# Weight forms of a pair kept in less space outside the FFN, and three more pairs in the 7-product form, in a streaming-encoder layer in split fp32

## The chip, the cores and the metric

The kernel runs on one core of one Trainium2 chip. The metric is the device time of one execution in microseconds (us). Before the change it is 1463.98 us, the median of three runs (1463.22 to 1464.94). One more execution was recorded by the profiler; it took 1464.63 us.

## What is computed

One layer of a hybrid encoder, with x of 256 rows (S) and 2048 columns (D), all in fp32. Cut to what matters:

```python
def reference(x, p, w_in, w_sb_out, w_ca_out, w_mix_out, rel_bias, g_mix, g_ffn, ...):
        h = rmsnorm(x, g_mix[i])
        proj = h @ w_in[i]
        q_sb, k_sb, v_sb, q_ca, k_ca, v_ca, gate_sb, gate_ca = jnp.split(proj, splits, axis=-1)
        y_sb = stick_breaking_attention(q_sb, k_sb, v_sb)
        y_ca = chunked_relpos_attention(q_ca, k_ca, v_ca, rel_bias[i])
        merged = (jax.nn.sigmoid(gate_sb) * (y_sb @ w_sb_out[i])
                  + jax.nn.sigmoid(gate_ca) * (y_ca @ w_ca_out[i]))
        x = x + merged @ w_mix_out[i]
        h = rmsnorm(x, g_ffn[i])
        g_ff, u_ff = jnp.split(h @ w_ffn_in[i], 2, axis=-1)
        x = x + (jax.nn.silu(g_ff) * u_ff) @ w_ffn_out[i]
        h = rmsnorm(x, g_ple[i])
        x = x + jax.nn.sigmoid(h @ w_ple_gate[i]) * (p[i] @ w_ple_in[i])
    return rmsnorm(x, g_final)
```

The two gates have 2048 columns each, w_mix_out is 2048 x 2048, and the FFN's hidden width is 5632.

## The kernel before

**Products in three parts.** Every operand of a big product is held as two fp32r tiles: hi, the value cast to fp32r, and lo, what the cast left over. A product is three matmuls (`three`, L267 to L270): hi·hi, hi·lo, lo·hi. The rows of x are the stationary operand, in tables T1, T2 or T3 of hi and lo by k-tile (128 rows of the contraction); the weights stream past in 512 columns. The weights arrive in fp32 in "raw" tiles of 128x1024, 512 KB each (L205, issued by SP in order, five buffers by turns, RAW = 5). ACT casts raw to hi (L239), DVE subtracts to get lo (`minus`, L221). There are three hi/lo buffers, and a fourth while the gates run (`extra`).

**Units.** A unit takes two blocks of 512 output columns over all k-tiles, two at a time: for 16 k-tiles, eight pairs. An ordinary pair is two pieces (one per block) of 12 matmuls each. A pair whose number is in `pairs` takes the 7-product form of a 2x2 block product (`pair_products`): seven products of three matmuls, 21 for 24. It needs extra forms of both sides. On the side of x these are sums of blocks of a table (`sums_of`), made once per table by `pair_sums` or by `into_table` and kept in FP (two slots before) or in a part of another tile (`F_gate`). On the side of the weights `split_pair` makes them for each pair: with raw1 and raw2 the raw tiles of the two k-tile rows, DVE makes t3 into xf, changes a block of raw2 in place, makes t2 and t4 into xf, and subtracts two lo of 1024 columns and one of 1536; ACT casts two hi and one of 1536 (L254, L257, L260). The 1536-wide hi and lo go to a "room" of 3072 columns. Four of the seven products are summed in PSUM tiles of their own (`su`). After the last such pair, `mid` adds those sums into the unit's output tile: one copy by ACT (L796) and four additions by DVE (L798), "su adds" here. At the unit's end `add_sums` (L802) adds the four PSUM tiles of the blocks, the "mm adds". Four mm tiles and two su tiles take turns, so the next unit's matmuls into one wait for the add that reads it.

**Stages.** The attention's projections and the two attentions come first. Then the gates: the first 512 columns of both as ordinary groups, then three units c=1, 2, 3, each with pairs 2, 4 and 6, all with one room, the tile that x had. Then the groups with w_sb_out and w_ca_out (the "out groups"), which multiply by the gates and put the sum into T1 (`into_table`, key "mg"). Then two mix units on w_mix_out, with pairs 4 and 6 only (MIX_PAIRS). Then the FFN in units with pairs 2, 4 and 6, the last norm's gate and the final norm.

**Order.** The program runs through `flush`: `prefetch` loads raw tiles as buffers come free and splits up to three pieces ahead; `tasks` are small jobs that are put between pieces. A scheduler then orders each engine's instructions ahead of time; on the chip each engine, SP's queue included, takes them strictly in that order. A raw tile's buffer is loaded again once the last instruction that reads it is done.

## Time and profile before

| what | value |
|---|---|
| median of three runs | 1463.98 us |
| profiled execution | 1464.63 us |
| its span, first to last instruction | 1462.9 us |
| TensorE's granted clock, mean | 0.998 |
| PE busy | 1450.5 us |
| DVE busy | 1211.8 us |
| ACT busy | 797.3 us |
| gate units c=1, c=2, c=3 | about 354 to 396, 396 to 438, 438 to 480 us |
| out groups, mix units, FFN | about 480 to 574, 574 to 655, from 655 us |

The profiled execution is 0.65 us above the median. PE is TensorE's matmuls, PEld its weight loads, DVE VectorE, ACT ScalarE, SP the queue that issues loads. In a timeline row the columns are start in us, duration in us, engine, line, operation, output<-inputs, shapes, the number of instructions that the row joins, and in brackets the idle time before it and what ended it. A row of a group gives count, busy us, mean ns of one, and idle time before by releaser. Matmuls overlap, so their durations are longer than the step from one start to the next.

### The profile page before, as it was taken

Reading aid. Unit: us, or ns where it says so; the run is one execution under the profiler, and the core shown is the slowest. Engines: PE = TensorE matmul, PEld = TensorE weight load, DVE = VectorE, ACT = ScalarE, POOL = GpSimd, SP = SyncE. Lnnn points to the kernel's source line nnn. Section 1 sums busy time; section 2 is a strip of 40 time slices with the busy share of each in tenths; the row PEclk is TensorE's granted clock in tenths of the full one; section 3 lists DMA queues with packets and bytes.
Section 4 is the critical chain, followed back from the end, with each engine's and each line's share of the span. In section 5 each row is a group of like instructions: output and inputs, shape, how many; then the busy total and the mean of one; then the engine's idle time right before and its main releaser. Section 6 shows DMA issues by size and latency. Waiting matters only on the chain.

```text
span 1462.9 us, 18648 instructions
## 1 busy us (share of the span) xinstructions
PE 1450.5 (99%) x6871; PEld 1214.2 (83%) x6871; DVE 1211.8 (83%) x1521; ACT 797.3 (55%) x949; POOL 23.5 (2%) x45
## 2 busy tenths in 40 slices
PE   9999999999999999999999999999999999999997
PEld 7888888888888888888888888888888888888886
DVE  5666667796888667988999999999999999999775
ACT  6455555457555444555555555555644555655652
POOL 0200000000000000000000000000000000000000
PEclk9999999999999999999999999999999999999999
DMA  9965555565666766666666566666666666666772
GB/s 297 294 186 173 173 173 176 179 194 160 214 196 206 236 189 190 207 191 183 188 189 203 184 205 203 200 211 210 192 191 213 188 203 194 207 203 200 235 230 97
DMA packets 164732, 291.19 MB, mean 199 GB/s; under 512 B 9024, under 2 KB 42096, under 8 KB 164384
## 3 DMA queue, kind: packets, MB, share of 16 engines
q1 hardware_dynamic: 162528, 281.32, 61.5%
q0 software_dynamic: 2112, 8.68, 1.9%
q8 instruction: 54, 0.88, 0.3%
q14 instruction: 38, 0.31, 0.1%
HBM read 284.19 MB, written 5.77 MB: 198 GB/s over the span
## 4 chain that ended last, share of the span: by engine, by line
PE 95%; DVE 2%; DMA 1%; issue 1%; ACT 0%; POOL 0%; POOLq 0%; DVEq 0%; ACTq 0%
PE mm L269 23%; PE mm L270 23%; PE mm L268 23%; PE mm L335 8%; PE mm L337 4%; PE su L268 3%; PE su L270 3%; PE su L269 3%; PE tp L413 1%; DMA raw<-in_w_ffn_out 1%; DVE lo L221 1%; DMA raw<-in_w_ple_gate 0%; PE warm L506 0%; PE yp L634 0%; PE xps L467 0%
## 5 line engine op out<-in xcount | busy, mean ns | idle before, releaser
L221 DVE TENSOR_TENSOR lo<-raw,hi 128x1024 fp32r<-128x1024 f32 (+1 forms) x517 | 626.8, 1220 | 147.0 <-ACT hi L239 144.0
L239 ACT CAST hi<-raw 128x1024 fp32r<-128x1024 f32 (+1 forms) x399 | 418.1, 1051 | 363.5 <-PE mm L270 233.7
L269 PE MATMUL mm<-lo,T 128*128 128x512 f32 x1391 | 542.7, 391 | 0.9 <-DVE lo L221 0.9
L270 PE MATMUL mm<-hi,T 128*128 128x512 f32 x1391 | 540.5, 390 | 0.0
L268 PE MATMUL mm<-hi,T 128*128 128x512 f32 x1391 | 516.8, 391 | 0.0
L269 PEld LDWEIGHTS mm<-lo,T 128*128 128x128 f32 x1391 | 261.2, 188 | 54.5 <-DVE lo L221 1.3
L270 PEld LDWEIGHTS mm<-hi,T 128*128 128x128 f32 x1391 | 261.2, 188 | 53.6
L268 PEld LDWEIGHTS mm<-hi,T 128*128 128x128 f32 x1391 | 261.0, 188 | 53.0
L335 PE MATMUL mm<-T,hi 128*128 128x512 f32 x512 | 180.3, 398 | 0.0
L337 PE MATMUL mm<-T,lo 128*128 128x256 f32 x512 | 141.0, 280 | 0.0
L257 ACT CAST hi<-raw 128x1024 fp32r<-128x1024 f32 x59 | 62.1, 1053 | 106.6 <-DVE raw L221 53.9
L335 PEld LDWEIGHTS mm<-T,hi 128*128 128x128 f32 x512 | 95.4, 188 | 21.5
L221 DVE TENSOR_TENSOR xf<-raw 128x512 f32<-128x512 f32 x118 | 81.1, 688 | 22.4 <-DMA raw<-in_w_in 5.6
L221 DVE TENSOR_TENSOR T<-xf,T 128x1536 fp32r<-128x1536 f32 x50 | 87.9, 1757 | 13.3 <-ACT T L260 12.8
L337 PEld LDWEIGHTS mm<-T,lo 128*128 128x128 f32 x512 | 96.3, 189 | 1.1
L260 ACT CAST T<-xf 128x1536 fp32r<-128x1536 f32 x50 | 74.1, 1481 | 30.0 <-DVE xf L221 29.8
L254 ACT CAST hi<-raw 128x1024 fp32r<-128x1024 f32 x59 | 62.1, 1053 | 22.5 <-PE mm L270 12.9
L798 DVE TENSOR_TENSOR C<-su,C 128x512 f32<-128x512 f32 x72 | 47.8, 685 | 4.6 <-PE su L270 3.2
L802 DVE TENSOR_TENSOR C<-mm,C 128x512 f32<-128x512 f32 x72 | 47.9, 684 | 2.8 <-PE mm L270 2.8
L221 DVE TENSOR_TENSOR xf<-raw,xf 128x512 f32<-128x512 f32 x59 | 40.5, 687 | 0.6
L221 DVE TENSOR_TENSOR raw<-raw 128x512 f32<-128x512 f32 x59 | 40.4, 685 | 0.2
L268 PE MATMUL mm<-T,T 128*128 128x512 f32 (+1 forms) x82 | 30.2, 368 | 0.0
(301 smaller groups left out, 1373.0 us busy)
## 6 DMA issues: line engine op xcount, KB each, us to landing
raw<-in_w_ffn_in SPq DMA_DIRECT2D x176, 512.0 KB, 4.2
raw<-in_w_in SPq DMA_DIRECT2D x160, 512.0 KB, 3.7
raw<-in_w_ffn_out SPq DMA_DIRECT2D x88, 512.0 KB, 4.8
raw<-in_w_mix_out SPq DMA_DIRECT2D x32, 512.0 KB, 4.4
raw<-in_w_ple_gate SPq DMA_DIRECT2D x32, 512.0 KB, 5.0
raw<-in_w_sb_out SPq DMA_DIRECT2D x16, 512.0 KB, 4.7
raw<-in_w_ca_out SPq DMA_DIRECT2D x16, 512.0 KB, 4.4
x<-in_x SPq DMA_DIRECT2D x4, 512.0 KB, 9.9
```

The lines of the kernel that those rows point to most:

```text
L221: nc.vector.tensor_tensor(out, a, b, ALU.subtract)
L239: nc.scalar.copy(hi[:, c : c + m], raw[:, c : c + m])
L254: nc.scalar.copy(h1, raw1)
L257: nc.scalar.copy(h2, raw2)
L260: nc.scalar.copy(xh, xf)
L268: nc.tensor.matmul(ps, xh, hi, start=a, stop=False)
L269: nc.tensor.matmul(ps, xh, lo, start=False, stop=False)
L270: state["mm"] = nc.tensor.matmul(ps, xl, hi, start=False, stop=z)
L335: nc.tensor.matmul(ps, hi[:, i, f], lhs[:, kt, :, :].rearrange("p c s -> p (c s)"), start=a, stop=False)
L337: nc.tensor.matmul(ps[:, :S], lo[:, i, f], lhs[:, kt, 0, :], start=False, stop=z)
L798: nc.vector.tensor_tensor(C[i], q, C[j], ALU.add)
L802: nc.vector.tensor_tensor(g["C"][i], g["ps"][i], g["C"][i], ALU.add)
```

## The change

While `late` has no pool, which is in the gates (the mix units and the FFN split their pairs with it, as before), `split_pair` works in less space. Only t3 goes to an xf of 512 columns; t2 and t4 overwrite the two blocks of raw1, once lo of raw1 is made, and raw1 as it then stands is cast and subtracted for the two extra forms; t3's forms have a tile x3 of 1024 columns. So one operation more is needed on DVE and on ACT per pair, and raw1 is read until the pair's last subtraction. The two raw tiles' blocks are named b11, b21, b12, b22. A room is then 3 x 1024 columns, and the gates get two by turns: thirds of `room`, and three tiles `more` in buffers that the attention has left. FP has three slots, the fourth set of forms is in the rest of `room`. With these, the mix units use pairs 2, 4 and 6, and gate unit c=3 uses pairs 1, 2, 4 and 6. The pending tasks are run before the sums for the gates, and those for pair 1 are a task.

```diff
-MIX_PAIRS = (4, 6)
+LAST_PAIRS = (1, 2, 4, 6)
...
-    FP = bp.tile([P, 2, 2, 4, P], F32R, tag="FP", name="FP")
+    FP = bp.tile([P, 3, 2, 4, P], F32R, tag="FP", name="FP")
...
+        if pool is not None:
+            xl, xh = room[:, :1536], room[:, 1536:]
+            xf = pool.tile([P, 1536], F32, tag="xf", name="xf")
...
+        else:
+            xh, xl, x3 = room
+            t3 = bp.tile([P, NB], F32, tag="xf", name="xf")
+            minus(t3, b22, b12)
+            minus(b12, b12, b11)
+            minus(l1, raw1, h1.bitcast(F32))
+            nc.scalar.copy(h2, raw2)
+            minus(b11, b22, b12)
+            minus(b21, b21, b11)
+            nc.scalar.copy(xh, raw1)
+            nc.scalar.copy(x3[:, :NB], t3)
+            minus(l2, raw2, h2.bitcast(F32))
+            minus(xl, raw1, xh.bitcast(F32))
+            minus(x3[:, NB:], t3, x3.bitcast(F32)[:, :NB])
...
+    while tasks:
+        run_task()
+    more = tuple(mp.tile([P, 1024], F32R, tag=tag, name="more") for tag in ("qT", "kT", "v"))
+    gate_rooms = [tuple(room[:, o : o + 1024] for o in (0, 1024, 2048)), more]
+    F_gate = dict(zip(PAIRS + (1,), F_gate))
+    for pair in PAIRS:
+        pair_sums(T1, 2 * pair, F_gate[pair])
+    tasks.append((None, lambda: pair_sums(T1, 2, F_gate[1])))
     for c in range(1, 4):
...
+             gate_rooms, lambda c=c: gate_slots(c), mid, add_sums, hneed, alone=True, pairs=PAIRS if c < 3 else LAST_PAIRS)
...
-                later(lambda: into_table(T1, c, mg, key="mg", forms=lambda kt: FP[:, kt // 4 - 2], pairs=MIX_PAIRS))
+                later(lambda: into_table(T1, c, mg, key="mg", forms=lambda kt: FP[:, kt // 4 - 1]))
...
-        unit(w_mix_out[0], (c * NB, (c + 1) * NB), range(KD), T1, lambda kt: FP[:, kt // 4 - 2], mix_rooms, C_slots,
-             mid, mix_post(c), lambda kt: ("mg", kt), pairs=MIX_PAIRS)
+        unit(w_mix_out[0], (c * NB, (c + 1) * NB), range(KD), T1, lambda kt: FP[:, kt // 4 - 1], mix_rooms, C_slots,
+             mid, mix_post(c), lambda kt: ("mg", kt))
```

Counted in the order lists, PE goes from 6828 to 6819 instructions, DVE has 36 more (10 in the mix units and 5 in their table, 6 in the new pair of c=3, 9 in the old gate pairs, 6 in pair 1's sums), ACT has 16 more. SP's loads keep their order and number. Up to the gates and in the last part of the kernel the lists are the same; from the gates to the end of the FFN they differ.

First place: pair 6 of gate unit c=2 on DVE, before. raw_3839 and raw_3841 are its two raw tiles; the other lo belong to pieces around it.

```order
L221 TENSOR_TENSOR xf_3888<-raw_3841 128x512
L221 TENSOR_TENSOR lo_2973<-raw_3785,hi_2972 128x1024
L221 TENSOR_TENSOR raw_3841<-raw_3841,raw_3839 128x512
L221 TENSOR_TENSOR lo_3890<-raw_3839,hi_3889 128x1024
L221 TENSOR_TENSOR xf_3888<-raw_3841 128x512
L221 TENSOR_TENSOR lo_3892<-raw_3841,hi_3891 128x1024
L221 TENSOR_TENSOR xf_3888<-raw_3839,xf_3888 128x512
L221 TENSOR_TENSOR room_2971<-xf_3888,room_2971 128x1536
L221 TENSOR_TENSOR lo_3920<-raw_3843,hi_3919 128x1024
```

The same pair after; its raw tiles are raw_3859 and raw_3861.

```order
L221 TENSOR_TENSOR xf_3913<-raw_3861 128x512
L221 TENSOR_TENSOR lo_2973<-raw_3803,hi_2972 128x1024
L221 TENSOR_TENSOR raw_3861<-raw_3861,raw_3859 128x512
L221 TENSOR_TENSOR lo_3909<-raw_3859,hi_3908 128x1024
L221 TENSOR_TENSOR room_2971<-xf_3913,room_2971 128x512
L221 TENSOR_TENSOR lo_3911<-raw_3861,hi_3910 128x1024
L221 TENSOR_TENSOR raw_3859<-raw_3861 128x512
L221 TENSOR_TENSOR raw_3859<-raw_3859 128x512
L221 TENSOR_TENSOR lo_3940<-raw_3863,hi_3939 128x1024
L221 TENSOR_TENSOR room_2971<-raw_3859,room_2971 128x1024
```

The 1536-wide subtraction became a 512-wide one early and a 1024-wide one at the end, which is the last to read raw_3859, and the lo of the next piece stands ahead of it. The buffer that it frees is raw_3957's, which the second place uses.

Second place: DVE at the end of unit c=2, before. gates<-su are the su adds, gates<-mm the mm adds of c=2; the raw tiles belong to c=3.

```order
L221 TENSOR_TENSOR lo_3966<-raw_3886,hi_3965 128x1024
L221 TENSOR_TENSOR lo_3970<-raw_3915,hi_3969 128x1024
L798 TENSOR_TENSOR gates_518<-su1_3790,gates_518 128x512 x2
L798 TENSOR_TENSOR gates_518<-su0_3789,gates_518 128x512 x2
L802 TENSOR_TENSOR gates_518<-mm0_3708,gates_518 128x512
L221 TENSOR_TENSOR xf_4043<-raw_3989 128x512
L802 TENSOR_TENSOR gates_518<-mm1_3709,gates_518 128x512
L221 TENSOR_TENSOR lo_3994<-raw_3917,hi_3993 128x1024
L802 TENSOR_TENSOR gates_518<-mm0_3722,gates_518 128x512
```

And after:

```order
L221 TENSOR_TENSOR xf_4032<-raw_3957 128x512
L221 TENSOR_TENSOR lo_3992<-raw_3937,hi_3991 128x1024
L221 TENSOR_TENSOR raw_3957<-raw_3957,raw_3955 128x512
L221 TENSOR_TENSOR more_3352<-xf_4032,more_3352 128x512
L816 TENSOR_TENSOR gates_518<-su1_3808,gates_518 128x512
L221 TENSOR_TENSOR xf_4079<-raw_4011 128x512
L816 TENSOR_TENSOR gates_518<-su1_3808,gates_518 128x512
L820 TENSOR_TENSOR gates_518<-mm0_3724,gates_518 128x512
L221 TENSOR_TENSOR raw_4011<-raw_4011,raw_4009 128x512
L221 TENSOR_TENSOR lo_4030<-raw_3955,hi_4029 128x1024
L816 TENSOR_TENSOR gates_518<-su0_3807,gates_518 128x512 x2
L221 TENSOR_TENSOR room_2971<-xf_4079,room_2971 128x512
```

Two xf, of c=3's pairs 1 and 2, and the work on their raw tiles stand ahead of and among the su adds. The four rows behind this piece are lo_2973<-raw_3957, raw_3955<-raw_3957, and the mm adds of mm1_3725 and mm1_3739.

Third place: PE at the start of unit c=3 after, nine matmuls from the second and then the eight behind them. Before, this stretch holds ordinary pieces only, into mm tiles; now pair 1's products stand in it.

```order
L286 MATMUL mm0_4044<-hi_3987,T1_71 128x512
L287 MATMUL mm0_4044<-lo_3988,T1_71 128x512
L288 MATMUL mm0_4044<-hi_3987,T1_71 128x512
L286 MATMUL mm0_4044<-hi_3987,T1_71 128x512
L287 MATMUL mm0_4044<-lo_3988,T1_71 128x512
L288 MATMUL mm0_4044<-hi_3987,T1_71 128x512
L286 MATMUL mm0_4044<-hi_4029,T1_71 128x512
L287 MATMUL su0_4091<-lo_4030,T1_71 128x512
L288 MATMUL su0_4091<-hi_4029,T1_71 128x512
```

```order
L287 MATMUL mm0_4044<-lo_4030,T1_71 128x512
L288 MATMUL mm0_4044<-hi_4029,T1_71 128x512
L286 MATMUL su0_4091<-hi_2972,room_2971 128x512
L286 MATMUL mm0_4044<-hi_4074,T1_71 128x512
L287 MATMUL su0_4091<-lo_2973,room_2971 128x512
L288 MATMUL su0_4091<-hi_2972,room_2971 128x512
L286 MATMUL su0_4091<-hi_4074,T1_71 128x512
L286 MATMUL mm1_4045<-hi_3987,T1_71 128x512
```

Matmuls on lo_4030 and lo_2973, the two lo that pair 1 needs, stand ninth and fifteenth in the unit; the first into mm0_4044 waits for the add that reads mm0_3724, and the one into mm1_4045 for the add that reads mm1_3725.

38 lines of the change are left out of this document (18 added, 20 removed).

## The prediction

> **What bounds the kernel now.** I read the page's busy line and chain first, then what PE waited for, then a table of stages, and last the rows of the places that the change touches.
>
> ```profile
> PE 1450.5 (99%) x6871; PEld 1214.2 (83%) x6871; DVE 1211.8 (83%) x1521; ACT 797.3 (55%) x949; POOL 23.5 (2%) x45
> PE 95%; DVE 2%; DMA 1%; issue 1%; ACT 0%; POOL 0%; POOLq 0%; DVEq 0%; ACTq 0%
> PE warm L506 <- POOL mhalf L97: 1.2, 1, 1.2
> PE mm L268 <- ACT hi L239: 1.2, 1, 1.2
> PE mm L269 <- DVE lo L221: 0.9, 1, 0.9
> ```
>
> PE is busy for 99% of the span and is 95% of the chain. It waits three times, 3.3 us in all. So there is no wait to win back here; only fewer matmuls can shorten the chain, and each new wait of PE lengthens it at full price. The stages (PE, PEld, DVE, ACT, POOL, then the granted clock, DMA share and GB/s) are gate units c=2 and c=3, the start of the mix, its second unit, and a stretch of the FFN:
>
> ```profile
> 396.00:438.00 42.00, 42.00 (x187) 34.77 (x186) 36.40 (x40) 24.22 (x25) 0.00 (x0) 1.00 0.66 203
> 438.00:480.00 42.00, 42.00 (x187) 34.80 (x186) 36.70 (x40) 24.18 (x24) 0.00 (x0) 1.00 0.64 202
> 574.00:608.00 34.00, 34.00 (x156) 28.25 (x155) 27.92 (x34) 18.63 (x20) 0.00 (x0) 1.00 0.61 192
> 608.00:655.00 47.00, 47.00 (x217) 39.09 (x216) 40.49 (x49) 28.40 (x39) 0.00 (x0) 1.00 0.65 203
> 800.00:900.00 100.00, 100.00 (x446) 82.83 (x445) 92.88 (x109) 52.70 (x53) 0.00 (x0) 1.00 0.64 209
> ```
>
> PE has no gap in any of them. DVE is the next resource: it has 5.60 us left of 42 in c=2, 5.30 in c=3, 6.08 of 34 at the start of the mix, and 7.12 of 100 in the FFN. All that the change adds, it adds to DVE and ACT.
>
> **What it takes away.** Three more pairs of k-tiles take the 7-product form: one in gate unit c=3, one in each mix unit. Each needs 7 × 3 = 21 matmuls in place of 24, so nine matmuls go; the order lists agree, 6819 PE instructions for 6828. What a matmul costs in a full stream is the step between starts, not its 0.39 us:
>
> ```profile
> 443.40 0.39 PE L268 MATMUL mm<-hi,T 128*128 128x512 f32 x1
> ...
> 445.22 0.39 PE L269 MATMUL mm<-lo,T 128*128 128x512 f32 x1
> ...
> 449.98 0.39 PE L270 MATMUL mm<-hi,T 128*128 128x512 f32 x1
> ```
>
> Between the last two lie 21 steps in 4.76 us, 0.2267 us each. The saving is 9 × 0.2267 = **2.04 us**, 0.14% of the time. By the full duration it would be 3.5; the rows exclude that. The Trainium skill's TensorE: Matmul & The Clock Gate, section Back-to-back issue gap, gives about 131 ns for a sustained matmul of 512 columns with its weight load; by it the saving would be 1.2 us, an estimate. No stretch here shows that pace, so the 0.2267 stands. I call a difference under 0.2% (2.93 us) no change, about what a measurement of this kernel can tell; the whole saving lies inside that.
>
> **What it adds on DVE.** These are the costs of the pieces, and next the steps between starts, at the end of unit c=2:
>
> ```profile
> L221 DVE TENSOR_TENSOR lo<-raw,hi 128x1024 fp32r<-128x1024 f32 x49 | 59.6, 1221 | 6.4 <-ACT hi L239 5.1 <-ACT hi L257 0.8
> L221 DVE TENSOR_TENSOR room<-xf,room 128x1536 fp32r<-128x1536 f32 x9 | 15.8, 1757 | 7.7 <-ACT room L260 7.7
> 431.40 1.76 DVE L221 TENSOR_TENSOR room<-xf,room 128x1536 fp32r<-128x1536 f32 x1 [1.62 <-ACT room L260]
> 433.07 1.22 DVE L221 TENSOR_TENSOR lo<-raw,hi 128x1024 fp32r<-128x1024 f32 x1
> 434.54 2.58 DVE L221 TENSOR_TENSOR lo<-raw,hi 128x1024 fp32r<-128x1024 f32 x2 [0.24 <-ACT hi L239]
> 438.83 2.73 DVE L798 TENSOR_TENSOR gates<-su,gates 128x512 f32<-128x512 f32 x4
> 441.48 0.68 DVE L802 TENSOR_TENSOR gates<-mm,gates 128x512 f32<-128x512 f32 x1
> 442.42 0.69 DVE L221 TENSOR_TENSOR xf<-raw 128x512 f32<-128x512 f32 x1 [0.25 <-DMA raw<-in_w_in]
> 443.02 0.69 DVE L802 TENSOR_TENSOR gates<-mm,gates 128x512 f32<-128x512 f32 x1
> 443.63 1.22 DVE L221 TENSOR_TENSOR lo<-raw,hi 128x1024 fp32r<-128x1024 f32 x1
> 444.76 0.69 DVE L802 TENSOR_TENSOR gates<-mm,gates 128x512 f32<-128x512 f32 x1
> 445.36 0.68 DVE L221 TENSOR_TENSOR raw<-raw 128x512 f32<-128x512 f32 x1
> 445.96 0.69 DVE L802 TENSOR_TENSOR gates<-mm,gates 128x512 f32<-128x512 f32 x1
> ```
>
> A 512-wide operation takes a step of 0.60, a 1024-wide 1.13, a 1536-wide 1.67. A new pair adds four 512-wide steps and the 1536-wide one, 4.07 us. In the nine old gate pairs the 1536 becomes 512 + 1024, 0.06 more each. By sums alone 4.07 fits into the 5.30 left in c=3 and the 6.08 left in the mix. What decides is DVE's order and what it waits for.
>
> **The end of gate unit c=2 (the main term).** Before, the four su adds run at 438.83 as soon as PE closes the sums, the mm adds follow, and one xf stands among them. The order lists (in the section on the change) put two xf there now, each waiting for a load, and the first stands ahead of all adds. That load takes the place of raw_3859, which is now read by the last operation of pair 6's split (before, the tile in its place was last read by the operation ahead of that). In the rows above that last operation and one lo end at 434.2; in either sequence of the two that is when the tile comes free. Loads then take:
>
> ```profile
> raw<-in_w_in SPq DMA_DIRECT2D x8, 512.0 KB, 4.5
> DMA to landing us min/median/max: 3.5/4.2/7.9
> ```
>
> The first row is the median over 425–446 us, the second the range over all three units. With 4.5, and 0.1 for the issue, xf_4032 starts at 438.8. DVE's queue from there: xf 0.60, lo 1.13, raw 0.60, room third 0.60, su add 0.60, xf_4079 0.60 (its load, behind the lo that ends at 437.1, has landed by 441.6), su add 0.60 and mm add 0.60, done at 444.2; raw 0.60 and lo_4030 1.13, done at 445.9; two su adds, a room third and lo_2973, done at 448.9; raw 0.60 and the next mm add, done at 450.1. PE, unheld, would start c=3 at 443.40. Its second matmul waits for that first mm add (0.6 us late), the ninth for lo_4030 (another 0.1), the fifteenth for lo_2973 (1.6) and the eighteenth for the next mm add (0.5). Sum: **2.8 us** of PE waiting. Each us by which the load lands sooner or later moves it by one: 1.8 with 3.5, 6.2 with 7.9, and 1.1 where no load is waited for at all, since DVE, free from 437.1, then sets the end by its work alone.
>
> **Gate unit c=1.** The 1024-wide lo of pair 4's extra forms now stands behind the xf of pair 6; before it stood ahead.
>
> ```profile
> 378.44 1.75 DVE L221 TENSOR_TENSOR room<-xf,room 128x1536 fp32r<-128x1536 f32 x1
> 383.01 0.69 DVE L221 TENSOR_TENSOR xf<-raw 128x512 f32<-128x512 f32 x1 [2.82 <-DMA raw<-in_w_in]
> 384.47 0.39 PE L269 MATMUL su<-room,FP 128*128 128x512 f32 x1
> ```
>
> Behind the xf it runs at 383.6 and ends at 384.8, where PE wants it at 384.47: **0.4 us**, 0 if the load comes 0.4 sooner, up to 3.7 more if it comes as late as the longest of the row above (7.9 against its median of 4.2).
>
> **The mix, the FFN, the rest.** At the start of the mix the smallest margin is a lo that ends at 600.5 and is used at 602.5:
>
> ```profile
> 599.30 1.22 DVE L221 TENSOR_TENSOR lo<-raw,hi 128x1024 fp32r<-128x1024 f32 x1
> 602.51 0.39 PE L269 MATMUL mm<-lo,T 128*128 128x512 f32 x1
> 896.69 0.69 DVE L221 TENSOR_TENSOR xf<-raw 128x512 f32<-128x512 f32 x1 [1.03 <-DMA raw<-in_w_ffn_in]
> ```
>
> A new pair's 4.07 meets 2.0 of margin, so at most 2.1 would reach PE; DVE's 6.08 of idle lies ahead of it in the same stretch, so I take **0.3**. Behind the mix, nine unit ends have an xf among the su adds (two before). The one at 896.69 waits 1.03 and PE, in the table, has no gap: **0**, up to 1.0 each if that cover is gone. The five extra operations of each table and pair_sums stand in the out groups and ahead of c=1, beside matmuls that use other tiles: 0. ACT is at 24 of 42; its 16 extra casts (about 1 us at most each) find idle time. SP's loads keep their order, only their release moves, counted above.
>
> **Sum.** 2.8 + 0.4 + 0.3 − 2.04 = +1.5. The profiled execution took 1464.63 (1462.9 of span and 1.7 around it), which gives 1466.1; it was 0.65 above the median of the runs, so the forecast on the median's scale is 1463.98 + 1.5 = **1465.4**.
>
> **The rivals.** *All covered*: loads land in 3.5, the sequence at c=2's end slides, and PE never waits. For it: 99% busy PE and the same kind of xf hidden at 896.69; against: a 12-step queue ahead of lo_4030 and lo_2973. Time: 1463.98 − 2.04 = 1461.9. *Slower, by the load behind the held tile*: the same place, with its load at 6.0 us or later. It decides from 2.04 + 2.93 = 4.97 us of waiting, which is 4.3 here beside the 0.7 elsewhere; with the 7.9 of the row it is 6.9, so 1463.98 + 4.9 = 1468.8. For it: three loads are let go within 3 us there, and share what moved 200 GB/s; against: the median is 4.5. PE's clock is 1.00 in every stage, and its longest wait 1.2 us. The Trainium skill's TensorE: Matmul & The Clock Gate, section HAM oscillation — how this bites in real kernels, says that idle gaps over some 3.4 us bring half the clock for a while; were one gap here that long, about 1.7 us more, an estimate that no run here shows. *Slower, by the unit ends behind the mix*: three of the nine show their 1.03, 3.1 in all, so +4.6, 1468.6. *Faster by over 0.2%* needs 0.9 us beyond the nine matmuls, for which no row speaks. That nothing is saved at all is excluded by the count.
>
> **How the numbers follow.** Forecast 0.49; all covered 0.24, of which 0.02 scatters below −2.93; the load 0.16; the unit ends 0.08; an unnamed gain 0.03. So faster 0.05, same 0.71, slower 0.24. The range runs from the covered case, 1461.6 with the runs' scatter, to the load's, 1468.8.
>
> **What would show it.** Right: in the changed profile PE waits two to four times near 444–450 us, 2 to 4 us in all, for gates (L820) and lo, with an xf that waits for a load ahead of the su adds; matmul steps stay 0.227. Wrong: no PE wait in the gates (then 1461.9), waits of over 4 us there, or waits of PE behind 650 us. The mix without waits would cost the forecast only 0.3.

## The result and the profile after

The changed kernel takes **1477.69 us** (median of five runs, 1477.14 to 1481.03), the kernel before in the same session 1464.46 (five runs, 1463.22 to 1464.96). The ratio is 1.0093, with a 95% interval of 1.0081 to 1.0104: slower by 13 us, and 9 us above the top of the predicted range. The profiled execution took 1477.37 us, with a span of 1475.7 for 1462.9. Of the experiments below, one execution of m9_pairs24 (1815.81 us) and one of b1_own_tile_second (2035.55 us) were far slower than all the others, and no figure uses them.

The page of the changed kernel, its busy line and its chain:

```profile
PE 1455.1 (99%) x6862; PEld 1209.9 (82%) x6862; DVE 1224.7 (83%) x1557; ACT 800.1 (54%) x965; POOL 23.7 (2%) x45
PE 71%; DVE 13%; DMA 9%; issue 4%; ACT 2%; SPq 0%; DVEq 0%; POOL 0%; POOLq 0%; ACTq 0%
```

PE's share of the chain went from 95% to 71%; DVE and loads took it over. PE's busy time rose although nine matmuls went: a matmul is shown for 0.39 us while the next starts after 0.2267, so up to 0.16 of each wait still counts as busy, and the first matmul after a wait shows as 0.47 to 0.51 us. What PE waited for, in all, times, longest (L816 and L820 of the changed kernel are the su and mm adds, L798 and L802 before):

```profile
PE mm L286 <- ACT hi L239: 2.9, 5, 1.2
PE mm L287 <- DVE lo L221: 1.8, 3, 0.8
PE warm L524 <- POOL mhalf L97: 1.2, 1, 1.2
PE su L286 <- ACT room L277: 1.1, 1, 1.1
PE mm L286 <- DVE gates L820: 1.0, 3, 0.4
PE mm L286 <- ACT hi L252: 0.9, 1, 0.9
PE mm L286 <- DVE C L816: 0.8, 2, 0.5
PE mm L286 <- ACT hi L259: 0.8, 2, 0.4
```

Three waits of 3.3 us before; now casts, lo and adds in many small waits. By stages (gate units c=2 and c=3, then the first mix unit in two cuts, then most of the second):

```profile
396.00:438.00 42.00, 41.19 (x181) 33.47 (x180) 38.08 (x44) 24.93 (x29) 0.00 (x0) 1.00 0.67 214
438.00:480.00 42.00, 39.69 (x170) 31.27 (x169) 36.71 (x46) 22.81 (x27) 0.00 (x0) 1.00 0.55 175
574.00:600.00 26.00, 25.56 (x117) 20.89 (x117) 20.25 (x25) 12.97 (x14) 0.00 (x0) 1.00 0.53 154
600.00:625.00 25.00, 23.16 (x94) 16.89 (x93) 18.80 (x19) 12.18 (x12) 0.00 (x0) 1.00 0.60 197
625.00:660.00 35.00, 33.38 (x152) 26.44 (x151) 31.78 (x42) 19.70 (x29) 0.00 (x0) 1.00 0.57 180
```

And the mix of the kernel before, in the same cuts:

```profile
574.00:600.00 26.00, 26.00 (x120) 21.63 (x119) 20.39 (x26) 14.88 (x16) 0.00 (x0) 1.00 0.60 189
600.00:625.00 25.00, 25.00 (x112) 20.70 (x111) 23.39 (x28) 13.91 (x19) 0.00 (x0) 1.00 0.68 218
```

The busy share hides a part of the loss, for the reason just given. The matmul counts show it: 94 for 112 in 600 to 625, 170 for 187 in c=3. So I add up, from the trace's PE rows, every step between two starts beyond 0.2267 us (steps over by 0.09 or more; no record is missing, since the counts of PE's records, 6871 and 6862, differ by the nine). Between 48 and 1360 us the kernel before loses 0.65 in this way, the changed one 15.5. The balance closes: 15.5 − 0.65 − 2.04 for the nine matmuls is 12.8, and the spans differ by 12.8. So nine matmuls were saved as predicted, and all the rest is waiting. "Lost time" below is this sum.

The place that the prediction was about, DVE at the end of gate unit c=2, after:

```profile
434.54 1.22 DVE L221 TENSOR_TENSOR room<-raw,room 128x1024 fp32r<-128x1024 f32 x1
...
441.23 0.69 DVE L221 TENSOR_TENSOR xf<-raw 128x512 f32<-128x512 f32 x1 [2.52 <-DMA raw<-in_w_in]
441.84 1.22 DVE L221 TENSOR_TENSOR lo<-raw,hi 128x1024 fp32r<-128x1024 f32 x1
...
444.18 0.69 DVE L816 TENSOR_TENSOR gates<-su,gates 128x512 f32<-128x512 f32 x1
...
445.98 0.68 DVE L820 TENSOR_TENSOR gates<-mm,gates 128x512 f32<-128x512 f32 x1
```

The last operation that reads pair 6's raw1 ends at 435.76, the load into that buffer is issued at 435.79 and lands at 441.20, the xf starts at 441.23, and the su and mm adds queue behind it. PE there:

```profile
446.21 0.47 PE L286 MATMUL su<-hi,T 128*128 128x512 f32 x1 [1.06 <-ACT room L277]
450.80 0.49 PE L286 MATMUL mm<-hi,T 128*128 128x512 f32 x1 [0.90 <-ACT hi L252]
452.58 0.50 PE L286 MATMUL mm<-hi,T 128*128 128x512 f32 x1 [0.23 <-DVE gates L820]
```

That is the predicted picture, 3.77 us of lost time for 2.8. Two of the releasers are not what they seem. The su add that frees the tile of the first matmul ended at 446.07, next to the cast named there (446.12). And the cast named at 450.80 could begin only at 449.70, when a matmul of PE let its buffer go; it costs nothing of its own, because lo_2973, which PE wants two matmuls later, came at 451.33. But two more places appeared: the end of unit c=1 (1.24), and the mix with 7.40 between 574 and 660. Of the first mix unit, DVE:

```profile
590.12 0.69 DVE L221 TENSOR_TENSOR FP<-work,FP 128x512 fp32r<-128x512 f32 x1 [0.69 <-ACT FP L419]
590.85 0.69 DVE L221 TENSOR_TENSOR xf<-raw 128x512 f32<-128x512 f32 x1
...
599.71 0.69 DVE L221 TENSOR_TENSOR xf<-raw 128x512 f32<-128x512 f32 x1
603.89 1.23 DVE L221 TENSOR_TENSOR lo<-raw,hi 128x1024 fp32r<-128x1024 f32 x1 [3.49 <-ACT hi L239]
605.04 0.68 DVE L221 TENSOR_TENSOR raw<-raw 128x512 f32<-128x512 f32 x1
```

ACT, which it waits for:

```profile
602.81 1.05 ACT L239 CAST hi<-raw 128x1024 fp32r<-128x1024 f32 x1 [5.56 <-DMA raw<-in_w_mix_out]
```

And SP's queue, which issues the loads, between 584 and 594:

```profile
SPq L205 <- DVE lo L221: 7.2, 2, 5.8
SPq L205 <- DMA raw<-in_w_mix_out: 2.4, 1, 2.4
```

Read these from the bottom. Pair 2's first subtraction (590.85) comes just behind the table's last FP subtraction (590.12), whose cast by ACT DVE had waited for. Pair 2's second raw tile (raw_5048), which it reads, had landed at 581.24. So two raw tiles of pair 2 and those behind it stay full, and SP, which has no free buffer, issues no load between 584.74 and 593.42. Then four go within 3.5 us (593.42 to 596.90) and take 3.86, 6.28, 6.95 and 7.07 us. One of them, an ordinary piece's, lands at 602.72; its cast is at 602.81, its lo at 603.89. That lo stands in DVE's order between the first and the second operation of pair 4 (599.71 and 605.04), so pair 4 waits as well. DVE is not overloaded there: it is busy for 18.80 of 25 us, less than before (23.39).

### The profile page after: what moved, and what is told of

The parts are those of the page before. It is cut to its first block, busy times and chain, and to the rows that moved or that the text cites. A ratio compares the mean times of both kernels' runs of the same rounds, so it can differ in the third digit from the quotient of the medians.

```text
span 1475.7 us, 18658 instructions
## 1 busy us (share of the span) xinstructions
PE 1455.1 (99%) x6862; PEld 1209.9 (82%) x6862; DVE 1224.7 (83%) x1557; ACT 800.1 (54%) x965; POOL 23.7 (2%) x45
## 4 chain that ended last, share of the span: by engine, by line
PE 71%; DVE 13%; DMA 9%; issue 4%; ACT 2%; SPq 0%; DVEq 0%; POOL 0%; POOLq 0%; ACTq 0%
PE mm L287 16%; PE mm L288 16%; PE mm L286 16%; PE mm L353 8%; DVE lo L221 6%; PE mm L355 4%; DMA raw<-in_w_ffn_out 3%; PE su L288 2%; PE su L287 2%; PE su L286 2%; DVE xf L221 2%; DMA raw<-in_w_ffn_in 2%; DMA raw<-in_w_mix_out 2%; DMA raw<-in_w_in 1%; PE tp L431 1%
## 5 line engine op out<-in xcount | busy, mean ns | idle before, releaser
L221 DVE TENSOR_TENSOR lo<-raw,hi 128x1024 fp32r<-128x1024 f32 (+1 forms) x517 | 624.5, 1219 | 156.0 <-ACT hi L239 148.1
L239 ACT CAST hi<-raw 128x1024 fp32r<-128x1024 f32 (+1 forms) x393 | 410.4, 1050 | 362.7 <-PE mm L288 186.7
L287 PE MATMUL mm<-lo,T 128*128 128x512 f32 x1370 | 534.8, 391 | 1.5 <-DVE lo L221 1.4
L288 PE MATMUL mm<-hi,T 128*128 128x512 f32 x1370 | 532.0, 390 | 0.0
L286 PE MATMUL mm<-hi,T 128*128 128x512 f32 x1370 | 514.7, 392 | 4.4 <-ACT hi L239 1.7
L286 PEld LDWEIGHTS mm<-hi,T 128*128 128x128 f32 x1370 | 257.0, 188 | 61.8 <-ACT hi L239 3.4
L287 PEld LDWEIGHTS mm<-lo,T 128*128 128x128 f32 x1370 | 257.3, 188 | 55.2 <-DVE lo L221 2.7
L288 PEld LDWEIGHTS mm<-hi,T 128*128 128x128 f32 x1370 | 257.2, 188 | 52.8
L221 DVE TENSOR_TENSOR xf<-raw 128x512 f32<-128x512 f32 x114 | 78.5, 688 | 28.9 <-DMA raw<-in_w_in 11.5
L259 ACT CAST hi<-raw 128x1024 fp32r<-128x1024 f32 x52 | 54.7, 1052 | 86.1 <-DVE raw L221 40.8
L221 DVE TENSOR_TENSOR T<-xf,T 128x1536 fp32r<-128x1536 f32 x52 | 91.3, 1756 | 9.3 <-ACT T L262 9.3
L262 ACT CAST T<-xf 128x1536 fp32r<-128x1536 f32 x52 | 77.1, 1482 | 35.0 <-DVE xf L221 34.9
L252 ACT CAST hi<-raw 128x1024 fp32r<-128x1024 f32 x62 | 65.1, 1050 | 20.0 <-PE mm L288 14.3
L221 DVE TENSOR_TENSOR raw<-raw 128x512 f32<-128x512 f32 x82 | 56.2, 686 | 0.5
L816 DVE TENSOR_TENSOR C<-su,C 128x512 f32<-128x512 f32 x72 | 47.8, 685 | 2.1 <-PE su L288 0.8
L820 DVE TENSOR_TENSOR C<-mm,C 128x512 f32<-128x512 f32 x72 | 47.1, 682 | 0.0
L221 DVE TENSOR_TENSOR xf<-raw,xf 128x512 f32<-128x512 f32 x52 | 35.7, 687 | 0.4
```

The costliest lines, as they stand in the source:

```text
L221: nc.vector.tensor_tensor(out, a, b, ALU.subtract)
L239: nc.scalar.copy(hi[:, c : c + m], raw[:, c : c + m])
L252: nc.scalar.copy(h1, raw1)
L259: nc.scalar.copy(h2, raw2)
L262: nc.scalar.copy(xh, xf)
L286: nc.tensor.matmul(ps, xh, hi, start=a, stop=False)
```

## The experiments

The theory after the result was this: in the gates, raw1, which is held until a pair's last subtraction, delays the next load; in the mix, a third pair in the first unit makes loads, and pieces that stand among others' work, late. The rival: DVE and ACT simply have too much to do. Times and ratios against the kernel before, and lost time in us by place ("gates" is 376 to 460 us, "mix 1" 574 to 625, "mix 2" 625 to 660, "FFN" 660 to 1360; between 460 and 574 only e3 lost 0.86, g1 1.21, t1 1.30, m7 0.72, m9 0.68, m5 0.38 and t2 0.10):

| kernel | gates | mix 1 | mix 2 | FFN | median | ratio (95%) |
|---|---|---|---|---|---|---|
| before | 0 | 0 | 0 | 0.2 | 1464.23 to 1465.11 by session | 1 |
| the change | 5.42 | 4.75 | 2.65 | 2.1 | 1477.69 | 1.0093 (1.0081 to 1.0104) |
| e1_gates_only | 5.58 | 0 | 0 | 0.2 | 1469.72 | 1.0033 (1.0021 to 1.0046) |
| e2_mix_only | 2.75 | 3.81 | 2.47 | 0.9 | 1474.30 | 1.0071 (1.0056 to 1.0086) |
| e3_lean_only | 2.53 | 0 | 0 | 0.2 | 1468.47 | 1.0028 (1.0017 to 1.0039) |
| g1_pair3 | 2.90 | 0 | 0 | 0.2 | 1468.18 | 1.0026 (1.0016 to 1.0036) |
| x2_own_tile | 0 | 0 | 0 | 0.2 | 1465.04 | 1.0004 (0.9995 to 1.0013) |
| x4_own_tile_146 | 2.07 | 0 | 0 | 1.5 | 1466.32 | 1.0012 (1.0003 to 1.0021) |
| m1_first46 | 5.58 | 0 | 0 | 0.5 | 1470.05 | 1.0042 (1.0027 to 1.0057) |
| m9_pairs24 | 3.78 | 0 | 0 | 0.2 | 1468.48 | 1.0026 (1.0016 to 1.0036) |
| m7_346 | 3.09 | 3.47 | 3.03 | 0.3 | 1474.49 | 1.0065 (1.0050 to 1.0080) |
| m5_table_early | 2.75 | 3.81 | 0 | 2.4 | 1473.25 | 1.0060 (1.0045 to 1.0075) |
| m8_forms6_late | 2.50 | 1.68 | 2.39 | 3.7 | 1473.15 | 1.0055 (1.0042 to 1.0069) |
| t1_mix_order | 3.34 | 3.03 | 5.02 | 0.9 | 1477.09 | 1.0079 (1.0063 to 1.0095) |
| t2_first_order | 2.85 | 2.38 | 1.84 | 2.2 | 1472.95 | 1.0060 (1.0046 to 1.0074) |
| b1_own_tile_second | 0 | 0 | 0 | 3.4 | 1466.46 | 1.0015 (1.0006 to 1.0024) |
| b2_own_tile_mix | 0 | 1.83 | 1.42 | 1.9 | 1468.90 | 1.0031 (1.0019 to 1.0042) |
| b3_mix_order | 0 | 3.49 | 4.81 | 0.5 | 1473.82 | 1.0060 (1.0047 to 1.0073) |
| b6_best | 0 | 1.63 | 2.24 | 3.6 | 1468.45 | 1.0027 (1.0017 to 1.0038) |
| b5_all_order | 0 | 3.49 | 4.91 | 41 | 1516.20 | 1.0351 (1.0337 to 1.0366) |

The lost time is that of one profiled execution each; b6's took 3.0 us more than its median, and x4's 1.7 more. The eight kernels with e3's code in the gates lose 2.5 to 3.8 there, so some tenths mean nothing. All edits below are against the changed kernel.

### Which part costs what

**e1_gates_only** keeps the gates as changed and gives the mix its two pairs (4, 6) back.

```diff
-                later(lambda: into_table(T1, c, mg, key="mg", forms=lambda kt: FP[:, kt // 4 - 1]))
+                later(lambda: into_table(T1, c, mg, key="mg", forms=lambda kt: FP[:, kt // 4 - 1], pairs=(4, 6)))
...
-             mid, mix_post(c), lambda kt: ("mg", kt))
+             mid, mix_post(c), lambda kt: ("mg", kt), pairs=(4, 6))
```

> The change without the third pair of the mix units (pairs 4 and 6 there, as before); the gates as changed. The trace of the changed kernel shows PE losing, by the steps between matmuls, 0.4 us in gate unit c=1, 1.2 at the end of c=1, 3.8 at the end of c=2, 7.3 in the mix units and about 2 behind them. Theory 'front of the mix' (the third pair stands first in each mix unit, takes two raw tiles at a time when the table's work holds DVE up, SP runs out of buffers, and later loads come only just in time): the mix loses under 0.5 us, the gates still 5.4, so 1468 to 1471 us. Rival 'less space' (the split in less space in the gates and the new order of the whole middle cost it, wherever pairs stand): the mix still loses 3 us or more, 1473 us or more.

**e2_mix_only** keeps the mix as changed and takes pair 1 out of the gates.

```diff
-             gate_rooms, lambda c=c: gate_slots(c), mid, add_sums, hneed, alone=True, pairs=PAIRS if c < 3 else LAST_PAIRS)
+             gate_rooms, lambda c=c: gate_slots(c), mid, add_sums, hneed, alone=True, pairs=PAIRS)
```

> The change without pair 1 in gate unit c=3 (pairs 2, 4 and 6 there); the mix units with their third pair. Theory 'front of the mix': the mix still loses 6 to 9 us, the end of c=2 now what the end of c=1 loses, about 1.2, so 1472 to 1476 us. Rival 'DVE falls behind in c=3 and the mix inherits it': the mix loses under 2 us, 1468 us.

**e3_lean_only** has both edits, so that no pair is new; only the smaller space and its order are left.

> Neither new pair: the split in less space, two rooms, three slots, and the pairs of before everywhere; no matmul saved. Theory 'front of the mix': what is left is 0.4 in c=1 and 1.2 at two unit ends, and 0 to 2 behind the mix, so 1466 to 1469 us. Rival 'less space': 1472 us or more. Second rival 'the split in less space costs nothing, the pairs all': 1464 to 1465 us.

Measured: 1.0033, 1.0071 and 1.0028. The smaller space alone costs 2.5 us of lost time in the gates with no pair added. Pair 1 brings the end of c=2 from 1.30 to 3.69. The mix costs 6.28 in e2, and nothing in e1 and e3, which have two pairs in its units. e1 loses in the gates what the change loses there (5.58 and 5.42), e2 in the mix 6.28 of the change's 7.40, so the parts act little on each other.

### The gates

**g1_pair3** makes pair 3 the fourth of c=3, in the middle of the unit instead of at its start; mix as before.

```diff
-LAST_PAIRS = (1, 2, 4, 6)
+LAST_PAIRS = (2, 3, 4, 6)
...
-    F_gate = dict(zip(PAIRS + (1,), F_gate))
+    F_gate = dict(zip(PAIRS + (3,), F_gate))
...
-    tasks.append((None, lambda: pair_sums(T1, 2, F_gate[1])))
+    tasks.append((None, lambda: pair_sums(T1, 6, F_gate[3])))
```

> Gates as changed, but c=3's fourth pair is pair 3 in place of pair 1; the mix units with pairs 4 and 6 only. With pair 1 the kernel lost 3.7 us at the end of c=2 against 1.1 to 1.3 in the two kernels whose c=3 has pairs 2, 4 and 6. Theory 'pair 1 brings its split, and its wait for a load, ahead of the su adds at the end of c=2': with pair 3 the end of c=2 loses 1.0 to 1.6, c=3 itself under 0.5, so about 2.5 us less than with pair 1: 1466 to 1468 us. Rival 'a fourth pair is too much work for c=3 wherever it stands': 3 us or more are lost in c=3 or at its ends, 1469 to 1471 us.

The end of c=2 falls to 1.20, what it costs without a fourth pair (e3: 1.30). So pair 1's own share, some 2.4, comes with its place at the front of the unit and not with there being a fourth pair. The loss of 1.21 between 460 and 574 is little more than e3's 0.86 there.

**x2_own_tile** gives t2 and t4 a tile of their own, so that raw1 is let go by its lo and its block subtractions; the second room goes for that. No new pair anywhere.

```diff
-            minus(b11, b22, b12)
-            minus(b21, b21, b11)
-            nc.scalar.copy(xh, raw1)
+            t24 = state["t24"]
+            minus(t24[:, :NB], b22, b12)
+            minus(t24[:, NB:], b21, t24[:, :NB])
+            nc.scalar.copy(xh, t24)
...
-            minus(xl, raw1, xh.bitcast(F32))
+            minus(xl, t24, xh.bitcast(F32))
...
-    more = tuple(mp.tile([P, 1024], F32R, tag=tag, name="more") for tag in ("qT", "kT", "v"))
-    gate_rooms = [tuple(room[:, o : o + 1024] for o in (0, 1024, 2048)), more]
+    state["t24"] = mp.tile([P, 1024], F32, tag="qT", name="t24")
+    gate_rooms = [tuple(room[:, o : o + 1024] for o in (0, 1024, 2048))]
```

> No new pair. The split in less space, but t2 and t4 go to a 1024-wide tile of their own (one of the attention's old buffers) and not over raw1, with one room; the rest as in the run with neither pair, which lost 0.2 in c=1 and 1.0 and 1.3 at the ends of c=1 and c=2. Theory 'raw1 held until the last subtraction lets its next load go late, and the xf that waits for it stands among the adds': the losses at the two ends fall under 0.5 each, 1464 to 1466 us. Rival 'the order, with an xf ahead of the su adds, costs it, whoever holds the tile': 1.0 or more at each end stay, 1466 to 1469 us.

Ratio 1.0004 (0.9995 to 1.0013). PE's waits in the whole kernel are those of before, and one of 0.2 us at 14 us:

```profile
PE warm L525 <- POOL mhalf L97: 1.2, 1, 1.2
PE mm L287 <- ACT hi L239: 1.2, 1, 1.2
PE mm L288 <- DVE lo L221: 0.8, 1, 0.8
```

Its DVE does as many operations as e3's (1536 in the whole kernel), and one room less is there to work in, yet all loss of the gates is gone. So the added work isn't the cause: that is shown. What is, is narrowed down but not proved, because x2 takes back several things at once: nothing is written over raw1 and raw1 isn't held, there is one room instead of two, and the order is another. In the changed kernel the rows above trace the held tile from its last reader to the late xf. In e3 the xf among the adds at the end of c=2 waits for a load into a buffer that an ordinary lo let go, at 439.08, and not raw1's last subtraction. In x2 the xf at the end of c=2 no longer waits, and it stands behind the su adds:

```profile
439.33 2.01 DVE L817 TENSOR_TENSOR gates<-su,gates 128x512 f32<-128x512 f32 x3
441.25 0.68 DVE L821 TENSOR_TENSOR gates<-mm,gates 128x512 f32<-128x512 f32 x1
441.85 0.68 DVE L221 TENSOR_TENSOR xf<-raw 128x512 f32<-128x512 f32 x1
```

**x4_own_tile_146** is x2 with pair 1 for pair 2 in c=3, which has three pairs then too: pair 1's place without the held tile.

```diff
-LAST_PAIRS = (1, 2, 4, 6)
+LAST_PAIRS = (1, 4, 6)
```

> The own tile and one room in the gates, the mix units with pairs 4 and 6; c=3 of the gates with pairs 1, 4 and 6, so pair 1 stands at the front of c=3 as in the change, but raw1 is free early. No matmul is saved. Theory 'the load behind the held raw tile makes the end of c=2 dear': the end of c=2 loses under 1.3 us in place of 3.7, 1464 to 1466 us. Rival 'an xf and pair 1's split among the su adds cost it, whenever the load comes': 2.5 us or more stay there, 1466.5 to 1469 us.

2.07 us at the end of c=2, all that the gates lose; this lies between the theory's 1.3 and the rival's 2.5. The xf of pair 1 stands there ahead of the su adds again and waits for its load, though no tile is held:

```profile
438.32 0.69 DVE L221 TENSOR_TENSOR xf<-raw 128x512 f32<-128x512 f32 x1 [2.15 <-DMA raw<-in_w_in]
...
440.67 0.69 DVE L817 TENSOR_TENSOR gates<-su,gates 128x512 f32<-128x512 f32 x1
...
444.20 0.68 DVE L821 TENSOR_TENSOR gates<-mm,gates 128x512 f32<-128x512 f32 x1
```

So the 3.7 at the end of c=2 have two parts: 2.1 to 2.4 come with pair 1's place, whose split stands among the adds, and the rest, 1.3 to 1.6, with the split that writes over raw1.

### The mix

**m1_first46** gives the first mix unit pairs 4 and 6, the second all three.

```diff
-             mid, mix_post(c), lambda kt: ("mg", kt))
+             mid, mix_post(c), lambda kt: ("mg", kt), pairs=(4, 6) if c == 0 else PAIRS)
```

> The changed kernel, but the first mix unit keeps pairs 4 and 6, the second has 2, 4 and 6; the table still makes the forms of pair 2. Theory 'front of the mix', where the trouble starts in the first unit beside the table's work: of the 7.3 us in the mix the first unit's 4.7 go and the second unit's 2.7 shrink to under 1.5, so 1471 to 1474 us. Rival 'three pairs are too many for the raw tiles in any mix unit': the second unit still loses 2.5 or more and the first nothing, 1473 to 1476 us.

Both mix units lose nothing, so a third pair in the second unit alone is free, and what the change loses between 625 and 660 depends on the first. DVE is busier there than in the changed kernel and PE has no gap:

```profile
600.00:625.00 25.00, 25.00 (x112) 20.69 (x111) 20.13 (x23) 12.80 (x13) 0.00 (x0) 1.00 0.68 215
625.00:660.00 35.00, 35.00 (x164) 29.14 (x163) 32.91 (x41) 22.20 (x33) 0.00 (x0) 1.00 0.54 171
```

**m9_pairs24** is e2 with pairs 2 and 4 in both mix units, in the table and in the unit.

```diff
-             mid, mix_post(c), lambda kt: ("mg", kt))
+             mid, mix_post(c), lambda kt: ("mg", kt), pairs=(2, 4))
```

> The mix units with pairs 2 and 4 only (as many pairs as before, but at the front), so the table's last part makes no forms and the late tiles do not wait for its work tile; c=3 of the gates with pairs 2, 4 and 6. Theory 'late tiles wait for the table': the mix loses under 1 us; the whole 1466.5 to 1469 us, as with neither pair. Rival 'pair 2 comes too soon behind the out groups, whatever holds its tiles': the mix loses 2 us or more, 1470 us or more.

No loss in the mix: pair 2 as such, the first behind the table, costs nothing when the unit has two pairs. The last part of the table makes no forms here, as in m8 below; m8, which has the third pair, loses 4.07.

**m7_346** is e2 with pairs 3, 4 and 6 in the mix. Pairs 3 and 4 follow each other in one room, so pair 3 is multiplied with pair 4's extra forms here.

```diff
-             mid, mix_post(c), lambda kt: ("mg", kt))
+             mid, mix_post(c), lambda kt: ("mg", kt), pairs=(3, 4, 6))
```

> The mix units with pairs 3, 4 and 6 in place of 2, 4 and 6, the table in its place, c=3 of the gates with pairs 2, 4 and 6. Pair 3 is used 24 matmuls (5.4 us) later than pair 2. Theory 'late tiles wait for the table': that is enough, the mix loses under 2 us, 1467 to 1470 us. Rival 'three pairs are more than the raw tiles carry': two pairs in a row make it worse, 6 us or more in the mix, 1473 to 1477 us.

6.50 lost, as much as with pair 2 (6.28), at other times. So the loss doesn't hang on pair 2. The run is a weaker witness than the others: no matmul on the extra forms runs in the first unit before 609.41, since pair 3's products wait for pair 4's forms too.

**m5_table_early** is e2 with the table's last part, c=3, asked for two pieces sooner.

```diff
-                later(lambda: into_table(T1, c, mg, key="mg", forms=lambda kt: FP[:, kt // 4 - 1]))
+                later(lambda: into_table(T1, c, mg, key="mg", forms=lambda kt: FP[:, kt // 4 - 1]), 1 if c == 3 else 3)
```

> The mix units with three pairs, c=3 of the gates with pairs 2, 4 and 6, and the last part of the mix's table (c=3) put two pieces earlier. All late tiles (xf, the room, the fourth hi and lo) lie in memory that is given free when that table's last operation on its work tile is done, so pair 2's split could not start before. Theory 'late tiles wait for the table': with the table two pieces (5.4 us) earlier, pair 2's split starts in time and the mix loses under 2 us in place of 6.3; in all 1467 to 1470 us. Rival 'three pairs in the first mix unit are more than five raw tiles carry, whenever the table is done': the mix still loses 4 us or more, 1472 to 1475 us.

The loss behind 600 is gone in full, but 3.81 appears at 590 to 595, where PE now waits for two casts that ACT does right behind the table's last one (the last section shows them).

**m8_forms6_late** is e2 with pair 6's forms made by a task that runs once the mix has begun, so that the table ends sooner.

```diff
-                later(lambda: into_table(T1, c, mg, key="mg", forms=lambda kt: FP[:, kt // 4 - 1]))
+                later(lambda: into_table(T1, c, mg, key="mg", forms=lambda kt: FP[:, kt // 4 - 1], pairs=(2, 4)))
...
+    tasks.append((None, lambda: pair_sums(T1, 12, FP[:, 2])))
```

> The mix units with pairs 2, 4 and 6, c=3 of the gates with pairs 2, 4 and 6. The forms of pair 6 are not made in the last part of the mix's table, with the old work tile, but by a task behind it in the late pool; so the late tiles (xf, the fourth hi and lo) no longer wait for that table's work tile, only for PE's transposes, some 3 to 4 us sooner. Three pairs stay in both mix units, with five raw tiles. Theory 'pair 2's split starts too late, because late tiles wait for the table': the mix loses under 2 us in place of 6.3, 1467 to 1469.5 us. Rival 'three pairs at the front of the first unit are more than five raw tiles carry': 4 us or more are lost in the mix, 1471 to 1475 us.

Pair 2's first operation is at 584.81 (590.85 in the changed kernel, 589.05 in e2), and the mix loses 4.07 for e2's 6.28. So an earlier end of the table is worth 2.2, and some 4 are not due to the wait behind it.

**t1_mix_order** is e2 with a rule for the scheduler in both mix units: the next piece's DVE operations go behind the last one of a pair's split, so that none stands inside it.

```diff
+                if "xl" in state and pc["g"].get("ext") is mix_rooms:
+                    with tc.issue_after(state["xl"].ins):
+                        split(pc)
```

> As the run with the mix units alone (pairs 2, 4 and 6 there; 2, 4 and 6 in c=3), but in the mix units DVE's lo of a piece that comes behind a pair may stand only behind the last subtraction of that pair. In the changed kernel's list such a lo stands inside the split of pairs 4 and 6, and its load goes out only when the pair before gives its raw tiles back, so the rest of the pair's split waits for it. Theory 'order': the mix loses under 2 us in place of 6.3, 1467 to 1470 us. Rival 'three pairs in the first unit are more than five raw tiles carry, in any order': 4 us or more are lost in the mix, 1472 to 1475 us.

The stretch from 600 to 625 loses nothing now, and the total rises: 3.03 ahead of it and 5.02 behind it. An order that helps one place takes operations that others wait for out of theirs.

**t2_first_order** has this rule only in the first unit, behind pairs 4 and 6.

```diff
+            if pc["g"] is state.get("mix0") and pc["kts"][0] >= 8:
+                state["xl"] = behind
...
+                if "xl" in state and pc["g"] is state["mix0"]:
+                    with tc.issue_after(state["xl"].ins):
+                        split(pc)
```

> As the run with the mix units alone, but the order rule holds only in the first mix unit and only behind pairs 4 and 6: no lo of a later piece may stand inside the split of pair 4 or 6. With the rule behind every pair of both units, PE lost nothing from 600 to 625 us (3.1 without it), but 3.0 at the split of pair 2 and 5.0 in the second unit, where the rule also held back lo that were due. Theory 'pair 2's late start, then a lo whose load is late inside the next pairs': 600 to 625 loses under 1 us, the second unit, which begins with more in hand, under 1, and only the 0.7 at pair 2 stays; in all the mix loses under 2.5 us, 1468 to 1471 us. Rival 'five raw tiles are too few for three pairs': 4 us or more stay in the mix, 1472 to 1475 us.

4.22 in the mix for e2's 6.28: a gain of 2.1, like m8's.

### Together

**b1_own_tile_second** is x2 with m1's mix (third pair in the second unit only), **b2_own_tile_mix** is x2 with m8's mix, **b3_mix_order** is b2 with t1's rule, **b6_best** is b2 with t2's, and **b5_all_order** is b2 with the rule behind every pair to the end of the FFN:

```diff
+                if "xl" in state:
+                    with tc.issue_after(state["xl"].ins):
+                        split(pc)
```

> t2 and t4 in a tile of their own with one room in the gates (pairs 2, 4 and 6 in all three units), the first mix unit with pairs 4 and 6, the second with 2, 4 and 6. What cost time in the gates is gone by the run with the own tile, what cost it in the mix by the run with 4 and 6 in the first unit; three matmuls (0.68 us) are saved. Theory 'raw1 held, and late tiles waiting for the table, are the two causes': PE loses under 0.5 us from 354 to 1300 us, 1463.5 to 1465 us, the same as before within 0.1%. Rival 'each kernel's order brings losses of its own': 1466 us or more.

> The own tile with one room in the gates, and three pairs in both mix units with the forms of pair 6 made late; six matmuls (1.36 us) saved. Theory 'raw1 held, and late tiles waiting for the table, are the two causes': PE loses under 2 us from 354 to 1300 us, all of it at the front of the mix, 1463 to 1465.5 us. Rival 'three pairs at the front of the first unit are more than five raw tiles carry': 1468 us or more.

> The own tile with one room in the gates, three pairs in both mix units, pair 6's forms made late, and the order of the last kernel in the mix units; six matmuls (1.36 us) saved. Theory 'order': PE loses under 1 us in the mix in place of 3.2, and what the rest of the order brings behind it (0 to 2), 1463 to 1466 us. Rival 'five raw tiles': 1467 us or more.

> All that the runs point to: the own tile and one room in the gates, pair 6's forms made late, the narrow order rule in the first mix unit; three pairs in both mix units, six matmuls (1.36 us) saved. Theory: PE loses under 1 us in the mix and 0 to 2 behind it, 1463 to 1466 us. Rival 'five raw tiles': 1467 us or more.

> As the kernel before it, with the same order behind every pair from the mix to the end. Theory 'order, in the FFN too' (the kernel with the second mix unit's pair alone lost 3.1 us in the FFN and none in the mix): PE loses under 1 us from 354 to 1300 us, 1463 to 1464.5 us. Rival 'the FFN's losses come of something else (an xf among the su adds that waits for its load)': 1 to 3 us are lost in the FFN, 1464.5 to 1467 us.

The gates lose nothing in any of the five, so x2's repair stands in other company. b1 saves three matmuls and loses nothing up to 660, but 3.4 in the FFN, whose code is the same; its ratio is 1.0015. b2 still loses 3.25 in the mix, and b6, which has t2's rule as well, 3.87: the two remedies don't add up. In b1, b2, b3 and b6 the time came out where the rival of the expectation put it, and not the theory. b5, 49 us above the higher of its forecasts, is the far miss of the study. The FFN's stretch of 700 us, and PE's longest sums of waits in it:

```profile
660.00:1360.00 700.00, 677.95 (x2952) 543.68 (x2951) 611.28 (x736) 357.40 (x386) 0.73 (x1) 0.99 0.59 186
```

```profile
PE su L288 <- DVE T L221: 9.8, 13, 0.8
PE su L287 <- ACT T L262: 7.7, 10, 1.4
```

PE waits above all for the extra forms of a pair (T, L221 and L262), 23 times up to 1.4 us. Why the rule makes those late was not followed further. No kernel beat the one before; x2 equals it, and has no new pair.

## Why the prediction was wrong

| term | predicted | measured (lost time) |
|---|---|---|
| nine matmuls | −2.04 | −2.04 (the balance closes with it) |
| inside gate unit c=1 | 0.4 | 0.41 |
| end of c=1 | not named | 1.24 |
| end of c=2 | 2.8 | 3.77 |
| mix | 0.3, at most 2.1 | 7.40 |
| FFN | 0 | 1.9 more than before |
| sum | +1.5 | +12.7 (spans: +12.8) |

**The step that failed is the mix term**: "A new pair's 4.07 meets 2.0 of margin, so at most 2.1 would reach PE; DVE's 6.08 of idle lies ahead of it in the same stretch". It set DVE's added work against the margin of one lo, took what was over as the upper bound, and went down to 0.3 because of DVE's idle time; the loads were not in it. In the run DVE did less between 600 and 625 us (18.80 us of 25, before 23.39) while PE lost 4.03 there, and 7.40 in the whole mix. What it leaves out is the way round: a pair whose split starts late keeps two raw tiles full, SP stops (no load for 8.7 us), the loads then land when they are wanted, and a piece whose load is last stands in DVE's order inside the next pair's split. m1 and m9 show that it takes a third pair in the first unit, and m7 speaks against its being pair 2. m8 and t2 show that the wait behind the table and the other piece's lo inside the split are worth about 2 each, but both together took away 2.4 (b6 3.87, for e2's 6.28). What holds the rest isn't settled. The rival that five raw tiles are too few for three pairs forecast the times of m5, m7, m8, t2, b2, b3 and b6, but no run had another number of raw tiles, so it is only argued.

**The end of c=2** was right in kind: an xf that waits for a load, ahead of the su adds, with PE waiting three times at 446 to 453. Two sizes were off. The tile came free at 435.76 instead of 434.2 (a lo ahead of its last reader had waited 1.02 for its cast), and the load took 5.4 instead of 4.5; so the xf came at 441.23 for 438.8. That pushed the first mm add from 444.2 to 446.7, but PE itself came 1.65 later, by what it had lost in c=1 and at its end; 3.77 were left. The held tile was named as the cause, and x2 agrees with that; that 2.1 of it come with pair 1's place alone (x4), the prediction had not separated.

**The end of c=1** loses with no new pair in it: there PE waited for two mm adds (0.45 and 0.36 of idle time, at 402.75 and 404.96).

```profile
394.73 4.62 DVE L221 TENSOR_TENSOR lo<-raw,hi 128x1024 fp32r<-128x1024 f32 x4
402.75 0.47 PE L286 MATMUL mm<-hi,T 128*128 128x512 f32 x1 [0.45 <-DVE gates L820]
403.61 0.69 DVE L221 TENSOR_TENSOR xf<-raw 128x512 f32<-128x512 f32 x1 [1.01 <-DMA raw<-in_w_in]
```

The second add stands behind the xf at 403.61, which waits for its load: the mechanism of c=2's end, one unit sooner. The first add has no load ahead of it. DVE had waited 1.12 for ACT's cast of the overwritten raw1, and then ran from 393.59 to 402.60 without a gap, with four lo and the su adds ahead of that add. The prediction worked out c=2's end only, because there two xf stand ahead of the adds; the three gate units share the way of splitting, so both ends should have been worked out. x2, which doesn't write over raw1, has 0 there.

**Inside c=1** the 0.41 for 0.4 is luck. The xf came at 384.71 and not at 383.01, so the lo behind it ran at 385.32 instead of 383.6; and PE wanted it not at 384.47 but nine places further on in its new order, at 386.29. The two misses cancel.

**The FFN**: the cover that the prediction named held in e1, e3, g1, m9 and x2, which lose the 0.2 of before, and failed by 0.1 to 3.5 us in the others (b5 apart). The code of the FFN is the same in all; what can differ is the order that the scheduler gives it. Which feature of that order costs the time isn't settled.

Two of the prediction's signs of being wrong came: more than 4 us lost in the gates (5.42), and waits of PE behind 650 us.

**The rivals**: the load behind the held tile, given 0.16, went as described, but with 5.4 us it stayed under the 6.0 from which it was to decide. Of the unit ends behind the mix, given 0.08, the trace shows one, 0.44 at 1165.6 with a wait for an su add; the rest of the FFN's loss lies elsewhere. No rival was about the mix.

## What to carry to other kernels

Where tiles are loaded by turns, the price of a new user is how long it keeps its tile full and what the load behind it then delays; that the new work fits into an engine's idle time is no bound until this has been counted. When a temporary is written over a loaded tile to save space, look for the load that waits for that buffer, in every unit that shares it: here a tile of 512 KB for two temporaries, in place of the second room, was worth all of 2.5 us. And where a scheduler orders engines ahead of time, a local gain is to be judged by the whole trace, since each edit brings an order of its own to places that it doesn't touch.
